# Attention passes of a two-layer decoder trunk: the second scores, the first maxima and the softmax scaling at other places in a hand-written order

## The chip, the cores and the metric

The kernel runs on one core of a Trainium2 chip. The metric is device time in microseconds (us) of one execution. The engines are named as in the profile: PE is the matrix engine and PEld its weight load, DVE the vector engine, ACT the scalar engine, POOL GpSimd, SP the engine that issues most loads.

## The reference

One sequence of 512 tokens, 1024 wide, goes through two layers. Layer 0 is a gated short convolution and a SwiGLU feed-forward part. Layer 1 is attention and the same kind of feed-forward part. The change touches the attention alone: 16 query heads of 64, four shared key/value heads, blocks of 128 queries that see their own block and the one before it, and a sink, one learned number a head that takes part in the softmax sum and not in the output.

```python
scores = einsum(q, k) / 8                      # per head: 4 blocks of 128 queries x 256 keys
scores = where(valid, scores, -1e30)           # sliding window of 128
probs = softmax(concat([scores, sink]))[..., :-1]
attn = einsum(probs, v) @ b_w_o
```

## The kernel before

All products are made in fp32 by splitting each operand into a high part (a rounded copy, made by ACT) and a low part (the difference, made by DVE), and adding three products: high times low, high times high, low times high. So each operand that PE multiplies costs one ACT and one DVE instruction, and each product three matmuls.

The attention works on head pairs: tile t of the queries holds heads 2t and 2t+1, and there are eight pairs. For one pair the steps are, with the letter that the order uses:

- **Q, R, H** project, rotate and split the queries (lines 1293 to 1305). The rotation reads PSUM on DVE (`sh`, `ra`, lines 1261 and 1263) and ends on POOL.
- **S0, S1** scores of the first and the second two query blocks (line 1319), twelve matmuls each, into two PSUM banks, one for each head of the pair.
- **M0, M1** maxima (line 1337): four DVE instructions each, that add the mask, write the scores `s` to SBUF and leave the negated row maximum in `nm`.
- **E00, E01, E10, E11** exponents (line 1353): four ACT instructions for each half, each with a read-out of its sum into `rs`, and two small ones with the sink's share `se`.
- **N0, N1** normalise (line 1371): DVE adds the sums, takes the reciprocal `rd` and multiplies the four pieces of `s` by it.
- **T0 to T3** turn (line 1384): PE transposes the probabilities into a PSUM bank `pt` of a pool of two. **P0 to P3** are the high copies `phi` or `lp` on ACT, **L0 to L3** the low parts `plo` or `lp` on DVE.
- **W0 to W3** weigh (line 1410): PE multiplies by the values into two banks `po`. **O** joins the two heads' results (line 1422: two ACT copies, then two DVE additions into `o`), and **o** splits the joined tile (line 1431: `ohl` or `ohi` and `olo`).
- **Z, z** work on the output projection of the first four pairs (line 1447: twelve matmuls into a bank `pe`, copied out by ACT). **G** and **g** split weights (`whi` on ACT, `wlo` on DVE).

The table ORDER (line 47) is walked once for each pass i of the loop at line 1539, i from 0 to 9. All instructions go to the engines' queues in the order in which the walk comes to them, each engine works off its queue in order, and an instruction at the head of a queue that waits holds up all behind it. In pass i, S, M, E and N work on pair i; T, P, L and W on pair i-1; a letter with a minus behind it (R-, O-, o-, H-) belongs to the pass before, so O- and o- work on pair i-2. Q works on pair i+2, R- and H- on pair i+1. Z starts in pass 5, when four pairs are joined, with two units in each of the passes 5 to 8, so that pass 5 has both the last Q and the first two Z. The passes 4 and 6 split more weights than the others.

NEXT (line 50) names the passes in which S1 is moved up to stand directly behind S0 (line 1548). There S1 takes its banks from the pool `ps_mm` of four, which also holds `pq`, `po` and `pe` (line 1322). In pass 5 and in pass 8 (which has no pair) it isn't moved; in pass 5, S1 stands behind P1 and reuses the two banks of `ps_sc` that M0 has read.

Of the kernel before, what the change touches and what calls it, by code (L numbers as in the profile page):

```python
# [10 lines left out]
F32 = mybir.dt.float32  # L11
F32R = mybir.dt.float32r
AF = mybir.ActivationFunctionType
ALU = mybir.AluOpType
PSUM = bass.MemoryType.PSUM

P = 128
# [27 lines left out]

EARLY_IN, REST_IN = 2, 0
ORDER = (
    "R- S0 T0 T1 O- Q0 M0 Q1 o- Z0 P0 P1 S1 T2 T3 L0 Q2 L1 G M1 E00 E01 k H- g0 Q3 P2 P3 E10 E11 Z1 z0 W0 L2 L3 A A A N0 W1 W2 N1 W3 g1 z1"
)
NEXT = (0, 1, 2, 3, 4, 6, 7)  # L50
STEP = {
    "S": "scores", "M": "maxima", "E": "exponents", "N": "normalise", "T": "turn", "P": "high",
    "L": "low", "W": "weigh", "O": "join", "o": "out", "Q": "project", "R": "rotate", "H": "split",
# [4 lines left out]
EARLY = 4  # L58
# [16 lines left out]
def yoco_kernel(  # L75
# [22 lines left out]
    nc = tc.nc  # L98
# [7 lines left out]
    small = ctx.enter_context(tc.tile_pool(name="small", bufs=3))  # L106
# [7 lines left out]
    def name(s):  # L114
        uid[0] += 1
        return f"{s}_{uid[0]}"
# [13 lines left out]
    def bank(s, pool=None):  # L130

        if pool is None:
            pool = (ps_mm, ps_sc, ps_mm, ps_pt)[turn[0] % 4]
            turn[0] += 1
        return pool.tile([P, S], F32, tag="bank", name=name(s))
# [421 lines left out]
    for l in range(2):  # L557
# [3 lines left out]
        for rd, (f0, f1) in enumerate(ROUNDS[:-1]):  # L561
            k = slice(f0 // 2, f1 // 2)
# [4 lines left out]
    def sum_on(at):  # L567

        issue(len(issues))
        if at in BEGIN:  # L570
            summing.append(sums_of[BEGIN[at]])
        for x in summing:
            x.step()
        summing[:] = [x for x in summing if x.steps]
# [390 lines left out]
    def first_weights(l):  # L965
        return ([w_gu[l, f, j] for f in range(2) for j in range(2)]
                + [w_gb[l, 0, b] for b in range(2)])
# [298 lines left out]
    def rope_turn(sh, eng):  # L1266
        eng.tensor_tensor(out=sh, in0=sh, in1=stab, op=ALU.mult)
# [10 lines left out]
    def rope_split(a, eng, large=False):  # L1278
        hi, lo = halves("rhl", F32R) if large else (slot("rhi", F32R), slot("rlo", F32R))
        nc.scalar.activation(hi, a, AF.Copy)  # L1280
        eng.tensor_tensor(out=lo, in0=a, in1=hi.bitcast(F32), op=ALU.subtract)
        return hi, lo
# [24 lines left out]
    class Heads:  # L1307
# [11 lines left out]
        def scores(self, half):  # L1319
            khi, klo = ks[self.t // 4]  # L1320
            qhi, qlo = qs[self.t].hi, qs[self.t].lo
            pool = ps_mm if half and self.t in NEXT else ps_sc
            self.pss[half] = pss = [bank("psc", pool) for _ in range(2)]
# [28 lines left out]

        def exponents(self, half, i):
            pe, nm = self.pe[half], self.nm[half]
            if i == 0:
                se = small.tile([P, 2, 2], F32, tag="se", name=name("se"))
                rs = small.tile([P, 2, 2], F32, tag="rs", name=name("rs"))
                self.sums[half] = se, rs
            se, rs = self.sums[half]
            cc = self.spans(half)[i][1]  # L1360
            for e in range(2):
                nc.scalar.activation(
                    pe[e][:, cc], pe[e][:, cc], AF.Exp, bias=nm[:, e, i : i + 1],
                    scale=-1.0, accum_out=rs[:, e, i : i + 1],
                )
            if i == 1:
                for e in range(2):
                    h = 2 * self.t + e
                    nc.scalar.activation(se[:, e], nm[:, e], AF.Exp, bias=snk[:, h : h + 1])

        def normalise(self, half):
            se, rs = self.sums[half]
            pe = self.pe[half]
            nc.vector.tensor_tensor(out=se, in0=se, in1=rs, op=ALU.add)
            rd = small.tile([P, 2, 2], F32, tag="rd", name=name("rd"))
            nc.vector.reciprocal(out=rd, in_=se)
            for i, cc in self.spans(half):
                for e in range(2):
                    nc.vector.tensor_scalar(
                        out=pe[e][:, cc], in0=pe[e][:, cc], scalar1=rd[:, e, i : i + 1],  # L1380
                        scalar2=None, op0=ALU.mult,
                    )
# [81 lines left out]
    with tc.manual_schedule(engines=ALL):  # L1464
# [20 lines left out]
        for hf in range(2):  # L1485
            c = slice(hf * 256, (hf + 1) * 256)
# [44 lines left out]
        for j in range(NB):  # L1531
            if j == 2:
                qs[0].split(nc.vector)
            nc.vector.tensor_tensor(out=dst[j][:, :, 1:3], in0=src[j],
                                    in1=dst[j][:, :, 0::3].bitcast(F32), op=ALU.subtract)

    with tc.manual_schedule(engines=ALL):
        sum_on("a0")
        for i in range(KT + 2):
            if i == KT:  # L1540
                res = Update(mix_o, B_ATT, [G_FPRE[1]])
                res.leaves = True
                ahead = Ahead(first_weights(1))
            if i == KT + 1:
                res.load()
            order = ORDER
            if i in NEXT:
                order = order.replace("S1 ", "").replace("S0 ", "S0 S1 ")
            for c in order.split():
                if c == "A":  # L1550
                    if i == KT:
                        ahead.one()
                    continue
                if c == "k":
                    if i == 3:
                        ks.append(rope_split(rot_k, nc.gpsimd))
                    continue
                late = c.endswith("-")
                op, n = c[0], [int(d) for d in c[1:].rstrip("-")]
                t = i - late  # L1560
                if op == "g":

                    u = 2 * (t - EARLY - 1) + n[0]
                    if u in (-2, -1, 2, 3):
                        j = u + 2 if u < 0 else u
                        early_w.append(split_weights(w_o[j // 2, j % 2], slots=j >= EARLY_IN))
                    continue
                if op in "SMENTPLWOo":
                    t -= op in "TPLWOo"
                    of = hp  # L1570
                elif op in "QRH":
                    t += LEAD
                    of = qs
                elif op == "G":
                    t += LEAD + 1
                    of = qs
                    if KT <= t < KT + 4:
                        j = t - KT
                        rest_w.append(split_weights(w_o[j // 2, 2 + j % 2], slots=j >= REST_IN))
                else:  # L1580
                    t = 2 * (t - EARLY - 1) + n.pop(0)
                    of = early
                if 0 <= t < len(of) and not (op in "RH" and t < LEAD - 1):
                    getattr(of[t], STEP[op])(*n)
                if op == "H" and i == 1:
                    rope_turn(begun_k[0], nc.gpsimd)
                if op == "H" and i == 2:
                    rot_k = rope_add(*begun_k, nc.gpsimd)
                if op in "RH" and i <= KT:
                    issue(len(issues) // 2 if op == "R" else len(issues))  # L1590
            if i <= KT:
                sum_on(f"a{i + 1}")
        close(rest_w, at, EARLY, res, ahead, lambda: sum_on(f"a{KT + 2}"), 1)
# [96 lines left out]
```

## Time and profile before

| what | value |
| --- | --- |
| median of 3 runs | 1024.36 us (1023.87 to 2562.63) |
| profiled execution, its time | 1024.8 us |
| its span | 1021.9 us (2.9 us lie around it) |
| PE busy | 1005.3 us, 98% of the span |
| DVE busy | 879.1 us, 86% |
| ACT busy | 589.6 us, 58% |
| POOL busy | 190.2 us, 19% |
| pass 0 begins (first `sh` of the walk) | 547.59 us |
| last W of the passes ends, first matmul of the part behind | 660.16 us |

The passes thus take 112.6 of the 1021.9 us. Ahead of them PE is busy without a gap, and behind them begins the rest of the output projection (`pmix`) and then the second feed-forward part. In the tables of the profile each row of a timeline has the start in us, the length in us, the engine, the line, the operation, the tile written and those read, the shape, and how many instructions were merged; a bracket behind a row is the time the engine stood idle before it and what ended that. A length includes the overlap with the next instruction, so what an instruction costs its queue is read from the start of one row to the start of the next.

### The profile page before, as it was taken

The numbers are of one execution on the slowest core, as the hardware profiler recorded it, in microseconds if no ns is written. First come the engines' busy times: TensorE is split into PE (matmuls) and PEld (weight loads), VectorE is DVE, ScalarE is ACT, GpSimd is POOL, SyncE is SP. The second block draws the span as 40 slices with busy tenths as digits, with TensorE's granted clock in tenths as the row PEclk, the third lists the DMA queues.
The fourth block names the chain that finished last, engine by engine and source line by source line (L and its number), as shares of the span: only waits on it lengthen the run. The fifth ranks groups of instructions, "written<-read, shape, count | busy, mean of one in ns | idle before, by whom it ended". The sixth has DMA issues, their size and how long they took to land.

```text
span 1021.9 us, 16136 instructions
## 1 busy us (share of the span) xinstructions
PE 1005.3 (98%) x5944; PEld 888.4 (87%) x5944; DVE 879.1 (86%) x1496; ACT 589.6 (58%) x1051; POOL 190.2 (19%) x251
## 2 busy tenths in 40 slices
PE   9999999999999999999999899999999999999997
PEld 8888888999889898998898777789998998989986
DVE  5766767899789989999879999888997899999896
ACT  6323445875655454656476678768566564645641
POOL 0443033112111111100114553221211010110001
PEclk9999999999999999999999999999999999999999
DMA  9897689559979699779405889976899676979742
GB/s 359 288 268 223 182 250 347 150 168 286 346 242 299 201 304 342 215 224 327 167 22 149 191 246 235 255 264 165 249 306 320 184 236 221 287 289 257 264 159 83
DMA packets 66575, 244.50 MB, mean 239 GB/s; under 512 B 7872, under 2 KB 8384, under 8 KB 54720
## 3 DMA queue, kind: packets, MB, share of 16 engines
q1 hardware_dynamic: 51328, 145.98, 38.4%
q0 software_dynamic: 14592, 96.48, 37.6%
q10 hardware_dynamic: 576, 1.02, 0.3%
q8 instruction: 46, 0.75, 0.3%
q14 instruction: 33, 0.27, 0.1%
HBM read 237.15 MB, written 102.76 MB: 333 GB/s over the span
## 4 chain that ended last, share of the span: by engine, by line
PE 91%; DVE 7%; ACT 2%; issue 0%; DVEq 0%; ACTq 0%
PE gx L1072 14%; PE gx L1075 7%; PE gz L195 4%; PE gz L193 4%; PE gz L194 4%; PE pcub L194 4%; PE pcub L193 4%; PE pcub L195 4%; PE px L194 4%; PE px L193 4%; PE px L195 4%; PE pmix L195 3%; PE pmix L193 3%; PE pmix L194 3%; PE gy L194 2%; PE gy L193 2%
## 5 line engine op out<-in xcount | busy, mean ns | idle before, releaser
L479 DVE TENSOR_TENSOR wlo<-raw,whi 128x1024 fp32r<-128x1024 f32 x225 | 274.7, 1225 | 53.0 <-ACT whi L478 52.8
L478 ACT ACTIVATE whi<-raw 128x1024 fp32r<-128x1024 f32 x225 | 233.7, 1051 | 100.4 <-DVE raw L466 28.8
L1072 PE MATMUL gx<-xt,whi 128*128 128x512 f32 x480 | 120.4, 393 | 0.0
L1072 PEld LDWEIGHTS gx<-xt,whi 128*128 128x128 f32 x480 | 86.2, 189 | 15.6
L547 POOL DMA_DIRECT2D hsum<-in_w_gb_dram x96 | 62.9, 734 | 152.9 <-ACT whi L478 90.0
L1034 DVE TENSOR_TENSOR st<-gx,st 128x256 f32<-128x256 f32 x200 | 78.0, 419 | 2.5 <-ACT st L1050 0.4
L1050 ACT ACTIVATE st<-gx 128x256 f32<-128x256 f32 x120 | 43.5, 380 | 62.3 <-PE gx L1075 58.6
L547 POOL DMA_DIRECT2D hsum<-hsum x32 | 25.4, 793 | 289.8 <-ACT whi L478 219.3
L1075 PEld LDWEIGHTS gx<-xt,wlo 128*128 128x128 f32 x480 | 65.5, 190 | 4.7
L1075 PE MATMUL gx<-xt,wlo 128*128 128x256 f32 x480 | 66.9, 282 | 0.0
L1086 ACT ACTIVATE gr<-gr 128x1024 f32<-128x1024 f32 x20 | 21.2, 1062 | 50.1 <-DVE gr L1034 50.1
L193 PE MATMUL px<-wlo,ahi 128*128 128x512 f32 x120 | 46.7, 389 | 0.0
L194 PE MATMUL px<-whi,ahi 128*128 128x512 f32 x120 | 46.7, 389 | 0.0
L195 PE MATMUL px<-whi,alo 128*128 128x512 f32 x120 | 46.7, 389 | 0.0
L195 PE MATMUL gz<-xhi,wlo 128*128 128x256 f32 x160 | 45.5, 284 | 0.0
L193 PE MATMUL gy<-xlo,whi 128*128 128x256 f32 x160 | 45.3, 283 | 0.0
L194 PE MATMUL gy<-xhi,whi 128*128 128x256 f32 x160 | 45.3, 283 | 0.0
L193 PE MATMUL gz<-xt,whi 128*128 128x256 f32 x160 | 45.3, 283 | 0.0
L194 PE MATMUL gz<-xt,whi 128*128 128x256 f32 x160 | 45.3, 283 | 0.0
L193 PE MATMUL gz<-xlo,whi 128*128 128x256 f32 x160 | 45.3, 283 | 0.0
L195 PE MATMUL gz<-xt,wlo 128*128 128x256 f32 x160 | 45.3, 283 | 0.0
L195 PE MATMUL gy<-xhi,wlo 128*128 128x256 f32 x160 | 45.3, 283 | 0.0
(293 smaller groups left out, 2969.5 us busy)
## 6 DMA issues: line engine op xcount, KB each, us to landing
hsum<-in_w_gb_dram POOLq DMA_DIRECT2D x96, 512.0 KB, 7.6
raw<-hsum SPq DMA_DIRECT2D x88, 512.0 KB, 8.0
raw<-in_w_gb_dram SPq DMA_DIRECT2D x60, 512.0 KB, 7.1
hsum<-in_w_dn_dram POOLq DMA_DIRECT2D x36, 512.0 KB, 8.1
raw<-in_w_dn_dram SPq DMA_DIRECT2D x32, 512.0 KB, 5.9
hsum<-hsum POOLq DMA_DIRECT2D x28, 512.0 KB, 5.7
raw<-in_w_in_dram SPq DMA_DIRECT2D x21, 512.0 KB, 7.4
hsum<-in_w_dn_dram POOLq DMA_DIRECT2D x12, 768.0 KB, 10.3
```

The costliest lines, as they stand in the source:

```text
L193: nc.tensor.matmul(out, whi, xlo, start=start, stop=False, **kw)
L194: nc.tensor.matmul(out, whi, xhi, start=False, stop=False, **kw)
L195: nc.tensor.matmul(out, wlo, xhi, start=False, stop=stop, **kw)
L478: self.begun = nc.scalar.activation(hi[:, :n], raw, AF.Copy)
L479: nc.vector.tensor_tensor(out=lo[:, :n], in0=raw, in1=hi[:, :n].bitcast(F32), op=ALU.subtract)
L547: nc.gpsimd.dma_start(dst, src, max_dma_last_dim=4 * 4 * S, **kw))
L1034: nc.vector.tensor_tensor(out=out, in0=a, in1=b, op=ALU.add)
L1050: nc.scalar.activation(ste, a, AF.Copy)
L1072: nc.tensor.matmul(banks[c][e], whi[:, kk], factors[p][k][2], start=opened and k == 0, stop=False, **kw)
L1075: nc.tensor.matmul(banks[c][e][:, :256], wlo[:, kk], factors[p][k][0], start=False, stop=k == 3 and p == 4, **kw)
L1086: nc.scalar.activation(kept[2], kept[2], AF.Silu)
```

## The change

Five edits, all in the attention passes:

1. NEXT is only pass 0. In the passes 1 to 4, 6 and 7, S1 now stands behind P1, with the banks of `ps_sc`.
2. O- (join) stands behind M0 instead of ahead of Q0 and M0, and o- (split of the joined tile) behind L0 instead of ahead of P0.
3. In the passes up to 5 the first output projection unit stands behind o- (as Y0) instead of ahead of P0. From pass 6 on it stays at Z0.
4. The sums `se`, `rs` and the reciprocal `rd` hold both halves of a pair in one tile of 128x8. N0 adds and inverts for both halves; N1 has no sum and no reciprocal of its own.
5. The four multiplications of the first half are ACT instructions with a scale operand; those of the second half stay on DVE.

```diff
--- before.py
+++ after.py
@@ -45,9 +45,9 @@
 
 EARLY_IN, REST_IN = 2, 0
 ORDER = (
-    "R- S0 T0 T1 O- Q0 M0 Q1 o- Z0 P0 P1 S1 T2 T3 L0 Q2 L1 G M1 E00 E01 k H- g0 Q3 P2 P3 E10 E11 Z1 z0 W0 L2 L3 A A A N0 W1 W2 N1 W3 g1 z1"
+    "R- S0 T0 T1 Q0 M0 O- Q1 Z0 P0 P1 S1 T2 T3 L0 o- Y0 Q2 L1 G M1 E00 E01 k H- g0 Q3 P2 P3 E10 E11 Z1 z0 W0 L2 L3 A A A N0 W1 W2 N1 W3 g1 z1"
 )
-NEXT = (0, 1, 2, 3, 4, 6, 7)
+NEXT = (0,)
 STEP = {
     "S": "scores", "M": "maxima", "E": "exponents", "N": "normalise", "T": "turn", "P": "high",
     "L": "low", "W": "weigh", "O": "join", "o": "out", "Q": "project", "R": "rotate", "H": "split",
@@ -1352,11 +1352,10 @@
 
         def exponents(self, half, i):
             pe, nm = self.pe[half], self.nm[half]
-            if i == 0:
-                se = small.tile([P, 2, 2], F32, tag="se", name=name("se"))
-                rs = small.tile([P, 2, 2], F32, tag="rs", name=name("rs"))
-                self.sums[half] = se, rs
-            se, rs = self.sums[half]
+            if half == i == 0:
+                self.sums = [small.tile([P, 2, 2, 2], F32, tag=s, name=name(s))
+                             for s in ("se", "rs")]
+            se, rs = (x[:, half] for x in self.sums)
             cc = self.spans(half)[i][1]
             for e in range(2):
                 nc.scalar.activation(
@@ -1369,13 +1368,19 @@
                     nc.scalar.activation(se[:, e], nm[:, e], AF.Exp, bias=snk[:, h : h + 1])
 
         def normalise(self, half):
-            se, rs = self.sums[half]
             pe = self.pe[half]
-            nc.vector.tensor_tensor(out=se, in0=se, in1=rs, op=ALU.add)
-            rd = small.tile([P, 2, 2], F32, tag="rd", name=name("rd"))
-            nc.vector.reciprocal(out=rd, in_=se)
+            if half == 0:
+                se, rs = self.sums
+                nc.vector.tensor_tensor(out=se, in0=se, in1=rs, op=ALU.add)
+                self.rd = small.tile([P, 2, 2, 2], F32, tag="rd", name=name("rd"))
+                nc.vector.reciprocal(out=self.rd, in_=se)
+            rd = self.rd[:, half]
             for i, cc in self.spans(half):
                 for e in range(2):
+                    if half == 0:
+                        nc.scalar.activation(pe[e][:, cc], pe[e][:, cc], AF.Copy,
+                                             scale=rd[:, e, i : i + 1])
+                        continue
                     nc.vector.tensor_scalar(
                         out=pe[e][:, cc], in0=pe[e][:, cc], scalar1=rd[:, e, i : i + 1],
                         scalar2=None, op0=ALU.mult,
@@ -1555,6 +1560,9 @@
                     if i == 3:
                         ks.append(rope_split(rot_k, nc.gpsimd))
                     continue
+                if c == ("Z0" if i <= EARLY + 1 else "Y0"):
+                    continue
+                c = c.replace("Y", "Z")
                 late = c.endswith("-")
                 op, n = c[0], [int(d) for d in c[1:].rstrip("-")]
                 t = i - late
```

The end of pass 3 (pair 3), DVE before: `se`, `rs` and `rd` are the sums and reciprocals, `s` the probabilities.

```order
L1374 TENSOR_TENSOR se_6199<-se_6199,rs_6200 128x4
L1376 RECIPROCAL rd_6241<-se_6199 128x4
L1379 TENSOR_SCALAR s_6151<-s_6151,rd_6241 128x128
L1379 TENSOR_SCALAR s_6152<-s_6152,rd_6241 128x128
L1379 TENSOR_SCALAR s_6151<-s_6151,rd_6241 128x256
L1379 TENSOR_SCALAR s_6152<-s_6152,rd_6241 128x256
L1374 TENSOR_TENSOR se_6224<-se_6224,rs_6225 128x4
L1376 RECIPROCAL rd_6256<-se_6224 128x4
L1379 TENSOR_SCALAR s_6193<-s_6193,rd_6256 128x256
L1379 TENSOR_SCALAR s_6194<-s_6194,rd_6256 128x256
L1379 TENSOR_SCALAR s_6193<-s_6193,rd_6256 128x256
L1379 TENSOR_SCALAR s_6194<-s_6194,rd_6256 128x256
```

DVE of the change at the same place:

```order
L1374 TENSOR_TENSOR se_6184<-se_6184,rs_6185 128x8
L1376 RECIPROCAL rd_6224<-se_6184 128x8
L1384 TENSOR_SCALAR s_6178<-s_6178,rd_6224 128x256
L1384 TENSOR_SCALAR s_6179<-s_6179,rd_6224 128x256
L1384 TENSOR_SCALAR s_6178<-s_6178,rd_6224 128x256
L1384 TENSOR_SCALAR s_6179<-s_6179,rd_6224 128x256
```

and ACT of the change, from the sink's exponents on:

```order
L1368 ACTIVATE se_6184<-nm_6177,snk 128x2 x2
L1381 ACTIVATE s_6117<-s_6117,rd_6224 128x128
L1381 ACTIVATE s_6118<-s_6118,rd_6224 128x128
L1381 ACTIVATE s_6117<-s_6117,rd_6224 128x256
L1381 ACTIVATE s_6118<-s_6118,rd_6224 128x256
L1431 ACTIVATE o_6297<-po_6215 64x512
L1431 ACTIVATE o_6297<-po_6216 64x512
L1409 ACTIVATE phi_6274<-pt_6269 128x512
L1409 ACTIVATE phi_6281<-pt_6276 128x512
L1441 ACTIVATE ohl_6335<-o_6297 128x512
```

Six DVE rows are gone, the one sum stands behind the exponents of both halves, and the first half's multiplications stand on ACT ahead of the two copies of the join; the split of the joined tile follows the two `phi` copies.

The start of pass 4 on DVE, before (the rotation, the join, and the first of the four maxima):

```order
L1261 STREAM_SHUFFLE sh_6266<-pq_6143 128x512
L1263 TENSOR_TENSOR ra_6268<-pq_6143,ctab_5215 128x512
L1428 TENSOR_TENSOR o_6317<-po_6232,o_6317 64x512
L1428 TENSOR_TENSOR o_6317<-po_6233,o_6317 64x512
L1346 ISA s_6330,nm_6329<-psc_6275,mask,nsnk 128x128
```

and of the change, from the third of the four maxima on (the rotation and the first two stand ahead of it):

```order
L1346 ISA s_6291,nm_6290<-psc_6255,mask,nsnk 128x256
L1346 ISA nm_6290 128x1
L1346 ISA s_6292,nm_6290<-psc_6256,mask,nsnk 128x256
L1346 ISA nm_6290 128x1
L1433 TENSOR_TENSOR o_6297<-po_6215,o_6297 64x512
L1433 TENSOR_TENSOR o_6297<-po_6216,o_6297 64x512
L1413 TENSOR_TENSOR plo_6275<-pt_6269,phi_6274 128x512
L1442 TENSOR_TENSOR ohl_6335<-o_6297,ohl_6335 128x512
L1413 TENSOR_TENSOR plo_6282<-pt_6276,phi_6281 128x512
```

The join `o` has moved from ahead of the four maxima to behind them, and the first low part `plo` from behind the split `ohl` to ahead of it.

PE in pass 5, before: the end of the first output projection unit (`pe`), and the start of S1.

```order
L193 MATMUL pe_6517<-wlo_6451,ohl_6514 128x512
L194 MATMUL pe_6517<-whi_6450,ohl_6514 128x512
L195 MATMUL pe_6517<-whi_6450,ohl_6514 128x512
L1334 MATMUL psc_6532<-rlo_6208,rhl_6386 128x256
L1334 MATMUL psc_6533<-rlo_6208,rhl_6386 128x256
```

The change has there S1's last matmuls, the transposes of T2 and T3 (`pt`), and behind them the start of the unit:

```order
L1334 MATMUL psc_6491<-rhi_6192,rhl_6366 128x256
L1334 MATMUL psc_6492<-rhi_6192,rhl_6366 128x256
L1396 MATMUL pt_6505<-ident,s_6352 128x128 x2
L1396 MATMUL pt_6505<-ident,s_6353 128x128 x2
L1396 MATMUL pt_6512<-ident,s_6352 128x128
L1396 MATMUL pt_6512<-ident,s_6353 128x128
L193 MATMUL pe_6519<-wlo_6375,ohl_5992 128x512
L194 MATMUL pe_6519<-whi_6374,ohl_5992 128x512
L195 MATMUL pe_6519<-whi_6374,ohl_5992 128x512
```

The unit stood ahead of S1, T2 and T3, and now stands behind them.

## The prediction

> **What bounds the kernel now.** I read the page first: the busy shares, then the chain that ended last.
>
> ```profile
> PE 1005.3 (98%) x5944; PEld 888.4 (87%) x5944; DVE 879.1 (86%) x1496; ACT 589.6 (58%) x1051; POOL 190.2 (19%) x251
> PE 91%; DVE 7%; ACT 2%; issue 0%; DVEq 0%; ACTq 0%
> ```
>
> PE bounds the program, and DVE holds 7% of the chain. The change touches only the attention passes, so next I cut the trace into passes, from one `sh` (or join) to the next. These are the passes 1 to 6; the columns are length, then busy time of PE, PEld, DVE, ACT and POOL with counts, then PE's granted clock.
>
> ```profile
> 556.55:567.08 10.53, 10.03 (x67) 8.61 (x66) 10.39 (x37) 8.95 (x28) 7.86 (x8) 1.00 0.83 206
> 567.08:581.08 14.00, 12.65 (x78) 10.94 (x78) 13.06 (x40) 9.58 (x29) 7.49 (x7) 0.88 0.84 207
> 581.08:594.21 13.13, 11.12 (x79) 9.56 (x78) 12.69 (x40) 10.11 (x31) 6.95 (x7) 1.00 0.83 169
> 594.21:610.06 15.85, 14.51 (x90) 12.62 (x91) 14.77 (x42) 11.59 (x31) 7.47 (x9) 0.89 0.80 250
> 610.06:622.59 12.53, 12.10 (x66) 9.67 (x65) 12.25 (x41) 8.91 (x30) 5.41 (x5) 1.00 1.02 312
> 622.59:639.05 16.46, 15.02 (x121) 13.00 (x119) 15.21 (x46) 14.33 (x39) 6.50 (x7) 1.00 0.91 209
> ```
>
> Here DVE is the fullest engine (12.69 of 13.13 us in pass 3), so its queue comes close to setting the pass. The waits of the same stretch (us in total, times, longest) tell what PE and ACT stand for:
>
> ```profile
> ACT ohl L1436 <- DVE o L1428: 12.3, 4, 3.7
> PE psc L1334 <- DVE ra L1263: 5.2, 3, 2.0
> ```
>
> S1 waits 5.2 us for the rotation (its second bank was `pq`'s). PE has other slack in these passes, so what counts is when DVE and ACT finish. Pass 3 on DVE, and then on ACT:
>
> ```profile
> 581.08 0.72 DVE L1261 STREAM_SHUFFLE sh<-pq 128x512 f32<-128x512 f32 x1
> 582.29 1.40 DVE L1428 TENSOR_TENSOR o<-po,o 64x512 f32<-64x512 f32 x2
> 583.72 0.35 DVE L1346 CUSTOM_DVE_ANT_0 s<-psc,mask,nsnk 128x128 f32<-128x128 f32 x1
> 585.08 0.69 DVE L1437 TENSOR_TENSOR ohl<-o,ohl 128x512 fp32r<-128x512 f32 x1
> ...
> 591.82 1.01 DVE L1379 TENSOR_SCALAR s<-s,rd 128x128 f32<-128x128 f32 x4
> 592.74 0.15 DVE L1374 TENSOR_TENSOR se<-se,rs 128x4 f32<-128x4 f32 x1
> 593.14 1.14 DVE L1379 TENSOR_SCALAR s<-s,rd 128x256 f32<-128x256 f32 x4
> 594.21 0.01 DVE L1261 LOAD_MASK_SELECT sh<-pq  x1
> ```
>
> ```profile
> 583.72 0.63 ACT L1436 ACTIVATE ohl<-o 128x512 fp32r<-128x512 f32 x1 [2.52 <-DVE o L1428]
> 584.26 1.07 ACT L1404 ACTIVATE phi<-pt 128x512 fp32r<-128x512 f32 x2
> 585.22 1.06 ACT L188 ACTIVATE whi<-raw 128x1024 fp32r<-128x1024 f32 x1
> 586.16 0.40 ACT L1362 ACTIVATE s<-s,nm 128x128 f32<-128x128 f32 x1
> ...
> 588.29 0.63 ACT L1280 ACTIVATE rhi<-ra 128x512 fp32r<-128x512 f32 x1
> 588.81 0.63 ACT L1280 ACTIVATE rhl<-ra 128x512 fp32r<-128x512 f32 x1
> 589.33 0.59 ACT L1404 ACTIVATE phi<-pt 128x512 fp32r<-128x512 f32 x1
> 590.07 0.51 ACT L1362 ACTIVATE s<-s,nm 128x256 f32<-128x256 f32 x1
> ...
> 592.55 1.21 ACT L1426 ACTIVATE o<-po 64x512 f32<-64x512 f32 x2
> ```
>
> ACT has no gap from the split of the joined tile (583.72) to the end of the second exponents (592.55), 8.83 us, and the second half's sum (592.74) follows at once. Two limits stand side by side: DVE's queue, and a ring through ACT. Until the second exponents are done, DVE fills its time with the first half's normalising (591.82 to 592.74 and its sum before).
>
> **The change part by part.** Edits 4 and 5 take six instructions a pair off DVE. In pass 3 the multiplications are 592.74 - 591.82 = 0.92 us, the sum and reciprocal 593.14 - 592.74 = 0.40: 1.32 us a pair, 10.6 us over eight. But the one sum now waits for the exponents of both halves, so DVE has nothing to fill that wait with: behind it in DVE's queue stand the second half's multiplications (T1 waits for them), the next rotation (POOL waits) and M0, and ACT's scaling and so T0 wait for its reciprocal. That is the wait the change adds. ACT gets four instructions with a scale operand. The nearest rows are one such instruction on 128x256 and an exponent on 128x128:
>
> ```profile
> 695.53 1.57 ACT L351 ACTIVATE xhl<-xt,gt 128x256 fp32r<-128x256 f32 x4 [0.67 <-PE xt L338]
> 586.46 0.20 ACT L1362 ACTIVATION_READ_ACCUMULATOR s<-s,nm 128x1 f32 x1
> ```
>
> Four of the first take 1.57, so about 0.37 each from start to start and a little over at the end; the second kind starts its read-out 0.30 after its own start at 586.16. Two of 0.37 and two of 0.29 make 1.32 us. From below, half a 128x512 copy (two `phi` in 584.26 to 585.22, so 0.24 for a half) gives 0.96 for four; from above, the whole first exponents with their read-outs and the sink's share, 586.16 to 588.29, give 2.13. I take 1.32, since the 128x256 row is the same kind of instruction.
>
> Now the ring of a pass in the change, from reciprocal to reciprocal, each link from the rows above: second half's multiplications 1.07 (593.14 to 594.21), rotation 1.21, maxima 1.36, join 1.43 (edit 2 puts the maxima into the ring), then on ACT split 0.54, `whi` 0.94, first exponents 2.13, `rhl` 0.52, `phi` and `lp` 0.74 (589.33 to 590.07), second exponents 2.48, and the sum and reciprocal 0.40. That is 12.82 us. The two `phi` copies (0.96) have left the ring, ahead of the split; the scaling (1.32) lies in the time in which ACT waits for the join, 2.52 us in the row at 583.72, and costs nothing there. If that cover were gone it would add its 1.32.
>
> - Pass 2: 14.00 becomes 12.82, -1.18.
> - Pass 3 has `rhi` as well (0.52): 13.34 for 13.13, +0.21.
> - Pass 1 has no join; its ring is scaling 1.32, T0 0.55 (half of eight transposes, 1.09 in a row below), `phi` 0.96, then 0.94 + 2.13 + 0.52 + 0.74 + 2.48 + 0.40, together 10.04 for 10.53: -0.49.
> - Pass 4 splits two more weights.
>
> ```profile
> 602.73 1.05 ACT L188 ACTIVATE whi<-raw 128x1024 fp32r<-128x1024 f32 x1
> 608.92 1.22 DVE L189 TENSOR_TENSOR wlo<-raw,whi 128x1024 fp32r<-128x1024 f32 x1
> ```
>
> The first adds 0.95 to the ring. The last `whi` now stands behind the scaling, and DVE's last `wlo` (1.14 to the next `sh`) waits for it: from the reciprocal 1.32 + 1.05 + 1.14 = 3.51 instead of 1.07, +2.44. Pass 4: 12.82 + 0.95 + 2.44 = 16.21 for 15.85, +0.36.
>
> So pass 5 starts 1.1 us earlier, at 608.95. Pass 5 is PE's:
>
> ```profile
> 616.15 0.87 PE L1391 MATMUL pt<-ident,s 128*128 128x128 f32 x6
> 616.78 0.47 PE L193 MATMUL pq<-xlo,whi 128*128 128x512 f32 x1
> 619.61 0.39 PE L193 MATMUL pe<-wlo,ohl 128*128 128x512 f32 x1
> 622.33 0.40 PE L1417 MATMUL po<-phi,vt 128*128 128x256 f32 x2
> 624.34 0.39 PE L1334 MATMUL psc<-rlo,rhl 64*128 64x256 f32 x2
> ```
>
> Before, the first unit filled PE while T2 and T3 waited for their `pt` banks. With edit 3 it stands behind T3, and T3's bank is free when L1 is done: rotation 1.21, maxima 1.36, join 1.43, then three DVE instructions of 0.6 (585.08 is the first of their kind), 5.8 us into the pass, 614.76. A third of the transposes 0.2, the unit 2.72, Q2 and Q3 2.83, the second unit 2.72 and W 2.01 end at 625.24, where before they ended at 624.34: +0.9. The lead of 1.1 is gone into PE's wait for L0 and L1, which is what comes late next. S1, which no longer stands behind S0, is made up later in the same pass. M0 waits for S0 and the join now stands behind M0. Pass 6 has the tail of pass 4 again (the last `whi` behind the scaling), +0.36; the passes 7 and 8 I take as even. Sum: +0.9 + 0.36 = +1.3 us.
>
> The profiled execution took 1024.8 us (span 1021.9 and 2.9 around it), the median shown is 1024.36; on it the forecast is 1025.7 us. With scaling at 0.96 or 2.13 the two tails move it by -0.7 or +1.6. The 5.2 us of S1's wait I count as no gain: PE then waits for the scaling instead, in the same slack. No moved step issues a DMA; the loads of weights, which SP issues when a `wlo` has freed a buffer, move with their pass by tenths of a us, and none is in the rows of waits that carry this sum.
>
> One edit is checked against a rule. These rows follow S1's waits of 1.84 and 1.34 us:
>
> ```profile
> 568.43 0.38 PE L1334 MATMUL psc<-rlo,rhl 64*128 64x256 f32 x1 [1.84 <-DVE ra L1263]
> 569.59 1.97 PE L1391 MATMUL pt<-ident,s 128*128 128x128 f32 x8
> ...
> 582.43 0.38 PE L1334 MATMUL psc<-rlo,rhl 64*128 64x256 f32 x1 [1.34 <-DVE ra L1263]
> 583.32 1.09 PE L1391 MATMUL pt<-ident,s 128*128 128x128 f32 x8
> ```
>
> After 1.84 us eight transposes took 1.97 us, after 1.34 us 1.09, and the granted clock of that pass is 0.88. The Trainium skill (TensorE: Matmul & The Clock Gate, section on the HAM clock gate) gives half rate only after an idle window of about 3.4 us. By that rule no wait here would slow PE and the slower rival below would have no price; the trace does not agree, and the sum goes by the rows.
>
> **The rivals.**
>
> *PE's new wait makes it slow (slower).* Behind the P3 copy S0 still needs two low parts (0.6 and half of that), a quarter of W (0.5) and its own matmuls (0.9, from 582.43 to 583.32), an estimate of 2.3 us; the scaling ends 2.48 + 0.40 + 1.32 = 4.2 us behind that copy. So T0 waits some 1.9 us, above the 1.84 that was followed by slow transposes. Each time costs 1.97 - 1.09 = 0.9 us. It decides only where PE is last, from pass 5 on; in four passes 3.5 us on top of the forecast: 1029.2. Against it: in pass 5 and 6 PE arrives late itself.
>
> *The lead of pass 5 is kept.* If the unit's delay is taken up because PE has slack behind it (12.10 of 12.53 busy in pass 5 speaks against that, 15.02 of 16.46 in pass 6 for it), the 1.1 us arrive: 1023.3.
>
> *DVE's queue alone was the bound.* Then its 10.6 us come in full: 1013.8. For it: DVE at 97% of pass 3. Against it: ACT's 8.83 us without a gap, into which the new sum runs.
>
> *The change does not do what it says*, in that S1 still waits: its banks are free after M0, 2.6 us into the pass, and PE comes to it after T0, T1, Q0 and Q1, later than that, so it hardly can be; and if S1 did wait as before, the time would be the ring's all the same, 1025.7, since S1's wait is counted at nothing. It has no chance of its own.
>
> **How the numbers follow.** Forecast 1025.7: 0.58. Slower 1029.2: 0.17. Lead kept 1023.3: 0.17. DVE alone 1013.8: 0.08. The range reaches from 1020.5 (short of the last) to 1029.5, which leaves out that case and about half of the slow one's upper side, under 2 in 10. The forecast's own range is 1024.5 to 1027. About 2%, 20 us, is what a measurement of this kernel can tell from no change; no case reaches it. Faster 0.01, within 0.98, slower 0.01.
>
> **What would show it.** Right: DVE busy about 868 us and ACT about 600; the wait of `psc` for `ra` gone; the sum (L1374) idle for ACT by about 2 us a pair; T0 waiting for ACT's scaling; passes 2 and 3 near 12.8 and 13.3 us; in pass 5 the transposes waiting for `plo`; the passes ending near 661.4. Wrong: passes of 11 us (the ring isn't closed by the sum), or transposes of 1.97 us in the passes 5 to 8.

## The result, and the profile after

The change took 1028.83 us, the median of five executions (1027.65 to 1030.66); the kernel before, run beside it, 1023.87. The ratio is 1.0052, with a 95% interval from 1.0035 to 1.0068: slower by 5.0 us. The forecast was 1025.7, 3.1 us less, and its range ended at 1029.5. That the kernel would be a little slower was right; the size, +1.3 us, was not.

The page's busy line of the kernel after:

```profile
PE 1007.9 (98%) x5944; PEld 886.4 (86%) x5944; DVE 868.9 (84%) x1448; ACT 601.9 (58%) x1083; POOL 189.6 (18%) x251
```

DVE lost 10.2 us of work and ACT gained 12.3, as the edits say. Next the passes 1 to 5, from `sh` to `sh`, and the sixth from its `sh` to the join of the seventh (length, then busy time of PE, PEld, DVE, ACT and POOL, then PE's clock):

```profile
558.75:569.31 10.56, 10.42 (x67) 8.68 (x69) 9.15 (x31) 9.36 (x32) 7.74 (x8) 1.00 0.86 216
569.31:582.17 12.86, 12.36 (x91) 10.07 (x89) 11.11 (x36) 11.08 (x35) 7.51 (x7) 1.00 0.83 214
582.17:595.55 13.38, 11.77 (x78) 9.37 (x78) 11.11 (x34) 11.60 (x36) 6.83 (x7) 1.00 0.79 176
595.55:611.97 16.42, 14.49 (x92) 11.44 (x93) 13.72 (x36) 14.60 (x39) 7.50 (x9) 1.00 0.82 252
611.97:625.31 13.34, 10.72 (x50) 8.27 (x49) 11.26 (x35) 10.42 (x34) 5.36 (x5) 0.87 1.03 290
625.31:647.23 21.92, 20.58 (x137) 17.14 (x136) 15.75 (x47) 16.45 (x45) 8.88 (x11) 1.00 0.73 177
```

Passes 2 and 3 are what the forecast said (12.82 and 13.34; in pass 3 no engine is busy for more than 11.8 of the 13.4 us), and pass 5 starts only 0.26 us earlier against pass 0 than before (62.21 us behind it, where it was 62.47). From there the time is lost. The first scores of pass 6 (S0, at 629.82) start 80.06 us behind pass 0, before 76.75, so 3.31 us; from S0 to the end of the span it is 399.08 us where it was 397.56, another 1.52. Together 4.83 us. All of it lies in the passes, which end 117.5 us behind pass 0 (at 667.24) where it was 112.6.

The span grew by 7.0 us, not 4.8, since pass 0 starts 2.2 us later (549.76 for 547.59). For the greater part that was lost near 285 us, in code that the change doesn't touch, where ACT waited for a load: this row stands among its waits, 5.3 us in two waits, the longer of 4.0 (a second execution of the same kernel, below, shows 3.1 and 2.6).

```profile
ACT whi L478 <- DMA raw<-hsum: 5.3, 2, 4.0
```

So the passes are measured from pass 0 on below. The waits in them (us in total, times, longest):

```profile
DVE se L1374 <- ACT se L1368: 8.7, 8, 1.6
ACT ohl L1441 <- DVE o L1433: 6.4, 4, 2.8
PE pt L1396 <- DVE plo L1413: 4.7, 7, 1.0
DVE s L1346 <- PE psc L1334: 4.2, 1, 4.2
PE pt L1396 <- ACT s L1381: 4.1, 10, 0.8
```

The wait of `psc` for `ra` is gone. The sum waits for ACT in each of eight pairs, about 1.1 us a pair. The fourth row is new: in pass 6 DVE stands 4.22 us at M0 until S0 has run, and the join stands behind it. DVE there:

```profile
630.84 0.35 DVE L1346 CUSTOM_DVE_ANT_0 s<-psc,mask,nsnk 128x128 f32<-128x128 f32 x1 [4.22 <-PE psc L1334]
...
632.19 1.41 DVE L1433 TENSOR_TENSOR o<-po,o 64x512 f32<-64x512 f32 x2
```

and ACT's half of that join:

```profile
629.82 1.21 ACT L1431 ACTIVATE o<-po 64x512 f32<-64x512 f32 x2 [1.20 <-PE po L1422]
```

It ended at 631.03, so the join could have begun there and began 1.16 us later. Pass 5 on PE, the second place where time goes:

```profile
614.37 0.76 PE L1334 MATMUL psc<-rlo,rhl 64*128 64x256 f32 x2 [0.94 <-DVE nm L1346]
...
616.73 0.66 PE L1396 MATMUL pt<-ident,s 128*128 128x128 f32 x4 [1.01 <-DVE plo L1413]
618.00 0.69 PE L1396 MATMUL pt<-ident,s 128*128 128x128 f32 x2 [0.61 <-DVE plo L1413]
618.34 0.78 PE L193 MATMUL pe<-wlo,ohl 128*128 128x512 f32 x1
...
622.38 0.39 PE L193 MATMUL pq<-xlo,whi 128*128 128x512 f32 x1
...
629.82 0.39 PE L1334 MATMUL psc<-rlo,rhl 64*128 64x256 f32 x2
```

PE stands idle three times within 4.6 us (613.43 to 618.00), then the unit's first matmuls take 0.78 and 0.63 us instead of 0.39, and the unit takes 4.04 us (618.34 to 622.38) where 2.72 was counted.

### The profile page after: what moved, and what is told of

Its sections match the earlier page's. It is cut to its first block, busy times and chain, and to the rows that moved or that the text cites. A ratio compares the mean times of both kernels' runs of the same rounds, so it can differ in the third digit from the quotient of the medians.

```text
span 1028.9 us, 16145 instructions
## 1 busy us (share of the span) xinstructions
PE 1007.9 (98%) x5944; PEld 886.4 (86%) x5944; DVE 868.9 (84%) x1448; ACT 601.9 (58%) x1083; POOL 189.6 (18%) x251
## 5 line engine op out<-in xcount | busy, mean ns | idle before, releaser
L194 PE MATMUL gz<-xhi,whi 128*128 128x256 f32 x160 | 45.3, 283 | 0.0
```

Source lines behind the costliest of these rows:

```text
L194: nc.tensor.matmul(out, whi, xhi, start=False, stop=False, **kw)
```

## The experiments

Three causes could account for the loss. Theory 1: the unit that was moved in pass 5 leaves PE idle there. Theory 2: the scaling on ACT with its one sum. Theory 3: the maxima ahead of the join. In this part edit 2 means the join behind the maxima alone, and the later place of the joined tile's split is counted with edit 3, since the unit needs the split. First, three kernels that undo one edit and one that makes one edit alone. For each kernel the table at the end gives the medians and three lengths from its trace.

### The unit and the split back at their places (edit 3 undone)

```diff
-Q0 M0 O- Q1 Z0 P0 P1 S1 T2 T3 L0 o- Y0 Q2
+Q0 M0 O- Q1 o- Z0 P0 P1 S1 T2 T3 L0 Q2
```

> The change, but with the split of the joined tile and the first output unit of pass 5 back at their old places, ahead of the first copies. Theory 1 (the loss is made in pass 5, where PE stands in front of the waiting transposes with nothing to do and its clock drops): the unit fills PE again, the transposes of pass 6 start 2.6 us earlier against the start of pass 0, so about 1026.2 us, and no matmul of the unit takes over 0.45 us. Theory 2 (the loss is made by the scaling on ACT with its one sum): no gain, 1028 to 1029. Theory 3 (maxima ahead of the join delays the join in the passes 6 to 8): no gain either, 1028 to 1029.

It took 1032.22 us (ratio to before 1.0092, 1.0077 to 1.0107): 9.0 us over the kernel before, where the change is 5.0 over it. All three expectations miss, theory 1's by its sign. It is half right all the same: pass 5, from `sh` to the S0 of the next pass, is 14.91 us instead of 17.85. But edit 3 also moves the split of the joined tile in every pass, and with the split early the passes 2 to 4 are 0.96 to 0.98 us longer each (13.84, 14.34 and 17.40), and the time from S0 of pass 6 to the end is 401.67 instead of 399.08. From pass 0 to the end this trace is 7.4 us over the kernel before; its pass 0 also starts 2.4 us later, behind code that no edit touches. The split ahead of the low parts holds up DVE and ACT until the join is done; with the join first it costs nearly as much (edits 2 and 3 undone together, below).

### The join ahead of the maxima (edit 2 undone for the join)

```diff
-T1 Q0 M0 O- Q1
+T1 O- Q0 M0 Q1
```

> The change, but with the join ahead of the maxima on DVE, as before. Theory 3 (in the passes 6 to 8 the maxima wait for scores that PE makes last, and the join, which is ready, stands behind them): the 1.2 to 1.4 us per pass come back in part, about 1027 us; the passes 2 to 4 get up to 1.36 us shorter each if ACT's ring holds them, and that lead is lost again at pass 5. Theory 1 (all in pass 5's unit): 1028 to 1029. Theory 2 (scaling on ACT with its one sum): 1028 to 1029.

It took 1023.69 us (ratio 1.0001, 0.9993 to 1.0010), no longer measurably slower than the kernel before. The loss is gone: theory 3, and more of it than theory 3 had expected. The passes 2 to 5 of this kernel:

```profile
567.75:579.32 11.57, 11.57 (x88) 9.74 (x88) 10.95 (x36) 10.97 (x35) 7.51 (x7) 1.00 0.92 241
579.32:591.41 12.09, 11.91 (x87) 9.80 (x83) 10.96 (x36) 11.49 (x36) 6.88 (x7) 1.00 0.88 176
591.41:606.54 15.13, 14.75 (x93) 11.62 (x93) 13.31 (x38) 14.48 (x39) 7.47 (x9) 1.00 0.84 249
606.54:619.62 13.08, 10.65 (x50) 8.57 (x49) 11.10 (x37) 10.53 (x34) 5.33 (x5) 0.87 1.02 325
```

Each of the first three is 1.29 us shorter than in the change, the four maxima's 1.34 us within 0.05 (570.54 to 571.88 in the change's pass 2). ACT's timeline in pass 2 says why. In the change:

```profile
573.32 0.63 ACT L1441 ACTIVATE ohl<-o 128x512 fp32r<-128x512 f32 x1 [1.17 <-DVE o L1433]
```

With the join first:

```profile
570.46 0.63 ACT L1441 ACTIVATE ohl<-o 128x512 fp32r<-128x512 f32 x1
570.99 1.06 ACT L188 ACTIVATE whi<-raw 128x1024 fp32r<-128x1024 f32 x1
571.93 0.40 ACT L1361 ACTIVATE s<-s,nm 128x128 f32<-128x128 f32 x1
```

ACT needs the join first (for the split) and the maxima two instructions later (for the first exponents). With the join first, DVE makes the maxima while ACT splits, and the exponents start without a wait. With the maxima first, ACT stands still for the join (1.17 us), and then the maxima have long been done. With the join first PE is busy in all of pass 2's 11.57 us, so that the ring alone sets this pass is not shown.

### Each half's sum and scaling back on DVE (edits 4 and 5 undone)

```diff
-            if half == 0:
-                se, rs = self.sums
...
+            se, rs = self.sums[half]
...
+            rd = small.tile([P, 2, 2], F32, tag="rd", name=name("rd"))
...
-                    if half == 0:
-                        nc.scalar.activation(pe[e][:, cc], pe[e][:, cc], AF.Copy,
-                                             scale=rd[:, e, i : i + 1])
-                        continue
```

> The moves of the change alone: each half has its own sum and reciprocal again and the first half is scaled on DVE. Theory 2 (one sum and scaling on ACT cost the time, by DVE's idle wait for the second exponents and by the late last weight split of the passes 4 and 6): 1024 to 1026 us. Theory 1 (pass 5's unit behind the transposes): 1028 or more, since DVE then carries 1.3 us more a pass while the transposes still wait for it.

It took 1027.18 us (1.0036, 1.0024 to 1.0048), between the two expectations: a loss of 4.0 us instead of 5.0, and 1.5 us less than the change from pass 0 to the end: theory 2 holds a fifth to a third of the loss, not all of it. Up to S0 of pass 6 this kernel is as slow as the change (79.90 us behind pass 0, the change 80.06); the gain lies behind that, 397.77 us to the end instead of 399.08.

### One sum and scaling on ACT alone (edits 4 and 5 on the kernel before)

```diff
+            if half == 0:
+                se, rs = self.sums
...
-            se, rs = self.sums[half]
...
-            rd = small.tile([P, 2, 2], F32, tag="rd", name=name("rd"))
...
+                    if half == 0:
+                        nc.scalar.activation(pe[e][:, cc], pe[e][:, cc], AF.Copy,
+                                             scale=rd[:, e, i : i + 1])
+                        continue
```

> The kernel before with one sum per pair and the first half's scaling on ACT, and none of the moves. Theory 1 (pass 5's unit): 1022.5 to 1024.5 us, no loss, since the unit stands where it stood. Theory 2 (one sum and scaling on ACT): 1027 to 1029, most of the loss.

It took 1025.55 us (1.0021, 1.0013 to 1.0030), between the two expectations. The passes 1 to 5 gain 1.8 us (S0 of pass 6 at 74.95 us instead of 76.75) and all behind loses 3.7 (401.26 instead of 397.56). So the two edits save time in the passes that DVE and ACT set, and cost more than that behind them, all of it in pass 7. There S1 waits for a bank until ACT has copied out the second unit of pass 6 (`mixo`), and this copy now stands behind the scaling. PE stands idle for 2.54 us. The kernel before has this wait, too, but of 1.01 us:

```profile
637.61 0.58 PE L1334 MATMUL psc<-rlo,rhl 64*128 64x256 f32 x1 [2.54 <-ACT mixo L1459]
```

```profile
634.54 1.49 ACT L1381 ACTIVATE s<-s,rd 128x128 f32<-128x128 f32 x4
635.95 1.13 ACT L182 ACTIVATE whi<-raw 128x512 fp32r<-128x512 f32 x2
636.98 0.57 ACT L1459 ACTIVATE mixo<-pe 128x512 f32<-128x512 f32 x1
```

From S0 of pass 6 to this S1 it is 15.07 us where it was 13.53. Behind the wait PE is slow (last section), and up to T2 of pass 7 it is 7.50 us where it was 5.31. Together these are the 3.7 us; from T2 on both kernels take the same 378.7. T0's waits for the scaling (0.52 us in all behind S0 of pass 6) are not the cost here. In the change S1 takes other banks and this wait does not come up, so the price of the edits there is another one.

### Edits 2 and 3 undone together

```diff
-T1 Q0 M0 O- Q1 Z0 P0 P1 S1 T2 T3 L0 o- Y0 Q2
+T1 O- Q0 M0 Q1 o- Z0 P0 P1 S1 T2 T3 L0 Q2
```

> Edits 2 and 3 undone together: join ahead of the maxima, and the joined tile's split and the first output unit at their old places; S1 late, one sum and scaling on ACT stay. Theory 3 as it now stands (the maxima ahead of the join sit in front of everything that hangs on the join, 1.36 us a pass): pass 5 then starts some 4 us earlier against pass 0 than before (ring 11.5, 12.0 and 14.9 to 15.1 us in the passes 2 to 4) and the unit fills PE there, 1019.5 to 1022 us. Rival (PE is full from pass 5 on, so that a lead at pass 5 is worth nothing): 1023 to 1024.

It took 1024.51 us (1.0007, 0.9998 to 1.0016), above both expectations. The lead of 4 us at pass 5 didn't come, only 1.4 (61.03 us for 62.47): the passes 2 to 4 were 12.48, 12.99 and 16.04 us, 0.90 to 0.91 longer each than with the split late. The ring worked out for the expectation had left out that the early split costs these passes, too. Pass 5 took 14.25 us to the next S0, as before. In pass 7 of this trace PE was slow behind a wait of 1.24 us (six transposes in 1.49 us, and a granted clock of 0.88 from 638.68 to 652.45).

### The maxima ahead of the join alone (edit 2 on the kernel before)

```diff
-T1 O- Q0 M0 Q1 o- Z0
+T1 Q0 M0 O- Q1 o- Z0
```

> The kernel before with edit 2 alone: the maxima ahead of the join, all else as before. Theory 3: most of the loss, 1027 to 1030 us, with the passes 2 to 4 up to 1.36 us longer each and the join of the passes 6 to 8 waiting behind maxima that wait for PE. Rival (the order of join and maxima costs only together with the late unit): 1023 to 1024.5.

It took 1029.64 us (1.0059, 1.0046 to 1.0072): the one edit alone loses 5.75 us, no less than all five. Its passes 2 to 5, and its row of ACT's wait for the join, 12.3 us in the kernel before:

```profile
566.84:581.30 14.46, 11.51 (x78) 9.50 (x78) 13.22 (x40) 9.46 (x29) 7.48 (x7) 1.00 0.75 191
581.30:595.78 14.48, 13.13 (x71) 11.40 (x73) 12.79 (x40) 9.24 (x29) 6.94 (x7) 0.76 0.72 153
595.78:612.22 16.44, 14.59 (x102) 12.01 (x99) 14.79 (x42) 12.10 (x33) 7.48 (x9) 1.00 0.81 247
612.22:626.11 13.89, 12.90 (x70) 10.00 (x69) 12.44 (x43) 9.45 (x30) 5.47 (x5) 1.00 1.00 293
```

```profile
ACT ohl L1436 <- DVE o L1428: 17.6, 4, 5.0
```

The four passes are 0.46, 1.35, 0.59 and 1.36 us longer. With the join first nothing of this is left, so edit 2's part for the join is shown as the cause from both sides: put in alone it costs 5.75 us, and taken out alone it lowers the loss from 5.0 or 4.7 to 0.5 us (by 5.3 us in the traces from pass 0 on). Two more pairs in the table at the end differ by it alone: the kernel with edits 1, 2 and 3 and that with 1 and 3 (5.3 us from pass 0 on), and the kernel without edit 3 and that with 1, 4 and 5 (6.2 us).

### The scaling behind the last weight split

The kernel is the one with edits 2 and 3 undone, with the scaling in a step X0 of its own.

```diff
-N0 W1 W2 N1 W3 g1 z1
+N0 W1 W2 N1 W3 g1 X0 z1
...
+        def scale(self, half):
+            pe, rd = self.pe[half], self.rd[:, half]
+            for i, cc in self.spans(half):
+                for e in range(2):
+                    nc.scalar.activation(pe[e][:, cc], pe[e][:, cc], AF.Copy,
+                                         scale=rd[:, e, i : i + 1])
```

> As the kernel with edits 2 and 3 undone, and the first half's scaling on ACT put behind the copy for the last weight split (whi) instead of ahead of it; it differs in the passes 4 and 6 alone. Theory (the late split is what the scaling costs in these two passes, 1.4 us each): DVE's wait of wlo for whi at their ends falls from 1.39 and 0.96 us to under 0.3, and the time by 0.5 to 2 us against that kernel. Rival (T0 waits for the scaling instead, and PE is what counts): no gain, or up to 1 us slower.

It took 1022.93 us (0.9992, 0.9983 to 1.0001), 1.6 us less than the same kernel without the step, within the expectation. Pass 4 fell from 16.04 to 14.56 us, the 1.4 us expected, and `wlo` no longer waits at the ends of the passes 4 and 6. Part of the gain goes into T0, which now waits up to 0.93 us for the scaling. The two traces differ by 2.23 us from pass 0 to the end: 0.78 up to S0 of pass 6 and 1.45 behind it. Behind it this kernel has no slow stretch in pass 7 (clock 1.00 from 637.66 to 650.17), so how much of the gain is the copy's place and how much PE's clock isn't separated.

### The change once more

> The change unaltered. If the 2.2 us by which pass 0 started later (549.76 for 547.59) belong to that one execution, pass 0 starts at 547.5 to 548.5 here and the median is 1027.5 to 1028.5 us; if they belong to the change, it starts at 549.8 again and the median is 1029 to 1030.5. In both cases pass 0's start to the end of the span takes 479 us, where it was 474.3 before.

The median was 1028.58 us (1.0042, 1.0028 to 1.0056). Pass 0 started at 548.46, between the two, and from there to the end took 479.44 us (before 474.31), so the passes' loss of 5 us repeats to 0.3, and the 2.2 us ahead of them belong to that one execution for the greater part.

### The join first from pass 5 on only

```diff
             order = ORDER
+            if i > EARLY:
+                order = order.replace("Q0 M0 O-", "O- Q0 M0")
```

> The change, with the join ahead of the maxima from pass 5 on and the maxima ahead of the join in the passes 1 to 4 as the change has it. Theory A (from pass 5 on PE is full, so what the passes 2 to 4 save or lose is worth nothing, and the loss of 5 us is made in the passes 5 to 8): pass 5 starts 62.2 us behind pass 0 as in the change, and the time is 1023.5 to 1025 us, as with the join first everywhere. Theory B (the 3.9 us that the passes 2 to 4 lose to the maxima come through): 1026 to 1027.5.

It took 1027.58 us (1.0039, 1.0027 to 1.0052): theory B, and 0.1 us over its bounds. Pass 5 starts 62.20 us behind pass 0, with the join first everywhere 58.34; of these 3.86 us 3.63 are still there at S0 of pass 6 (79.56 and 75.93) and 3.56 at the end. A lead at pass 5 does come through; PE has waits there to give up. So of the 5.34 us that the join behind the maxima costs, 3.56 are made in the passes 1 to 4 and 1.78 from pass 5 on.

### Edits 1 and 3 alone

Against the change, beside the sums and the scaling as shown for the third kernel:

```diff
-T1 Q0 M0 O- Q1
+T1 O- Q0 M0 Q1
```

> The kernel before with edit 1 (second scores late) and edit 3 (the joined tile's split and the first output unit late) alone: join ahead of the maxima, each half with its own sum, first half scaled on DVE. Theory (edits 4 and 5 cost 1.2 to 1.9 us by the late weight splits and the idle wait of the one sum): 1021.5 to 1023 us, under the 1023.7 of the kernel with the join first. Rival (the one sum and the scaling on ACT are what pays for the late unit, since DVE is then 1.3 us a pass fuller): 1024 to 1026.

It took 1022.22 us (0.9986, 0.9977 to 0.9995), as the theory said. Beside the kernel with the join first it shows edits 4 and 5 once more: up to S0 of pass 6 they save 0.18 us, behind it they cost 1.57 (397.87 for 396.30).

### The join first, and the scaling behind the split

```diff
-T1 Q0 M0 O- Q1 Z0 ... W3 g1 z1
+T1 O- Q0 M0 Q1 Z0 ... W3 g1 X0 z1
```

> Edits 1, 3, 4 and 5 with the join ahead of the maxima, and the first half's scaling behind the copy for the last weight split. Theory (the two parts add up): 1.5 us under the 1023.7 of the kernel with the join first, so 1021.5 to 1022.5 us. Rival (PE has no room from pass 5 on and S1's wait for the first maxima, 2.38 us in pass 5, holds the time): 1023 to 1024.

It took 1020.59 us (0.9973, 0.9964 to 0.9982), 2.9 us faster than the kernel before and the best of all: the parts add up, and to more than expected: some 3 us under the kernel with the join first (2.80 in the traces) rather than 1.5. Pass 4 gives 1.48 of them, and pass 5 to the next S0 another 1.16 (S1 waits 0.62 us for the maxima there, in the other kernel 2.38, and PE's granted clock is 1.00 there, in the other kernel 0.87). The end of pass 4 in it, on DVE and on ACT:

```profile
602.28 0.20 DVE L1376 RECIPROCAL rd<-se 128x8 f32<-128x8 f32 x1
602.52 1.14 DVE L1382 TENSOR_SCALAR s<-s,rd 128x256 f32<-128x256 f32 x4
603.58 1.22 DVE L189 TENSOR_TENSOR wlo<-raw,whi 128x1024 fp32r<-128x1024 f32 x1
604.73 0.01 DVE L1261 LOAD_MASK_SELECT sh<-pq  x1
```

```profile
601.95 1.05 ACT L188 ACTIVATE whi<-raw 128x1024 fp32r<-128x1024 f32 x1
602.90 1.48 ACT L1391 ACTIVATE s<-s,rd 128x128 f32<-128x128 f32 x4
```

The copy runs while DVE makes the sum, and the low part follows the multiplications at once. In the change the same place reads:

```profile
608.29 1.14 DVE L1384 TENSOR_SCALAR s<-s,rd 128x256 f32<-128x256 f32 x4
610.82 1.23 DVE L189 TENSOR_TENSOR wlo<-raw,whi 128x1024 fp32r<-128x1024 f32 x1 [1.39 <-ACT whi L188]
```

### A quarter of the projection ahead of the second scores

```diff
-O- Q0 M0 Q1 Z0 ... Y0 Q2 L1
+O- Q0 M0 Q1 Q2 Z0 ... Y0 L1
```

> As that kernel, with the third quarter of the next query projection (Q2, 1.36 us on PE) ahead of the second scores, where PE waits 2.38 us for the first maxima in pass 5. If that wait is on the path that sets the end, the time falls by about 1.4 us more, to 1020 to 1021; if not, it stays within 0.5 us of that kernel. In the passes 1 to 4, where the second scores wait little, Q2 ahead of them can delay the transposes by up to 1.36 us; if those counted, it would be slower by 1 to 3 us.

It took 1020.76 us (0.9977, 0.9968 to 0.9986), the same time, which both first readings of the expectation allow. That decides little: pass 1 grew by 1.3 us (11.81 for 10.52) and pass 5 to the next S0 shrank by as much (15.07 for 16.43), so a gain and a loss cancelled. The expectation had named each of them, and not both together. The move in pass 5 alone was not run, nor was the version that these lengths point to, split late in all passes but early with its unit in pass 5.

### All kernels

"Loss" is the median less that of the kernel before on the same chip. The other columns are us from the traces: start of pass 5 behind pass 0, start of S0 of pass 6 behind pass 0, and from there to the end of the span.

| kernel | median | loss | pass 5 | S0 of pass 6 | from there |
| --- | --- | --- | --- | --- | --- |
| before | 1023.87 | | 62.47 | 76.75 | 397.56 |
| all five edits | 1028.83 | 5.0 | 62.21 | 80.06 | 399.08 |
| all five, again | 1028.58 | 4.7 | 62.22 | 80.31 | 399.13 |
| without 3 | 1032.22 | 9.0 | 65.13 | 80.04 | 401.67 |
| join first (1, 3, 4, 5) | 1023.69 | 0.5 | 58.34 | 75.93 | 397.87 |
| join first from pass 5 | 1027.58 | 4.1 | 62.20 | 79.56 | 397.80 |
| 1, 2, 3 | 1027.18 | 4.0 | 61.82 | 79.90 | 397.77 |
| 4, 5 | 1025.55 | 2.3 | 60.67 | 74.95 | 401.26 |
| 1, 4, 5 | 1024.51 | 0.6 | 61.03 | 75.28 | 400.20 |
| 1, 4, 5, scaling late | 1022.93 | -1.0 | 59.57 | 74.50 | 398.75 |
| 2 | 1029.64 | 5.8 | 64.87 | 79.80 | 400.05 |
| 1, 3 | 1022.22 | -1.2 | 58.42 | 76.11 | 396.30 |
| 1, 3, 4, 5, scaling late | 1020.59 | -2.9 | 56.83 | 73.26 | 397.74 |
| the same with Q2 early | 1020.76 | -2.7 | 58.30 | 73.37 | 397.64 |

Read along one path, the 4.83 us come apart: edits 1 and 3 give 1.90 (0.64 up to S0, 1.26 behind), edits 4 and 5 on top cost 1.39 (-0.18 and +1.57), and the join behind the maxima on top of these costs 5.34 (4.13 and 1.21). The shares hold for this path: put on the kernel before alone, edits 4 and 5 cost 1.90 in the traces (-1.80 and +3.70) and edit 2 costs 5.54. Edits 1 and 3 were not run apart.

## Why the prediction was right or wrong

**The bound, ACT's ring: right.** Passes of 12.82 and 13.34 us were forecast for the passes 2 and 3, 12.86 and 13.38 came, and without the maxima in the ring (11.46 and 11.98 by the same rows) 11.57 and 12.09. The four scalings take 1.40 us on ACT where 1.32 was taken (608.35 to 609.75), and in the passes 2 and 3 they lie in ACT's idle time, as said. The sum's wait for ACT came as 1.1 us a pair and not 2.

**Pass 1: wrong by 0.5 us.** The step gave 10.04 by the ring; PE is busy 10.42 of the 10.56 us that came. PE's share of that pass had stood in the rows shown (10.03 of 10.53). With 0.2 us more at the end of pass 4 (16.42 for 16.21), the lead at pass 5 was 0.26 us and not 1.1.

**Pass 5: right in the order of events, too small in its size.** The step gave +0.9 us at S0 of pass 6; +3.31 came. Of the 2.4 us between, 0.84 are the lead that wasn't there, 0.36 T2's and T3's later start and length, and 1.32 the unit at a slow clock; Q2 and Q3 gave back 0.1. The slower rival had that price of a wait, but put it at T0, which waited 0.4 us on average, 0.8 at most (4.1 us in ten waits), and was not slow. Nor does a wait above 1.84 us always make PE slow (last section). Its 1029.2 is near the result by chance: it counted four passes, and one was hit.

**S1's bank: wrong in the word "hardly".** In pass 5 S1 did wait for the maxima, 0.94 us. T2 and T3 waited for `plo` in any case, so this wait can have cost time only as a part of PE's idle time ahead of the slow unit; no run shows that by itself.

**Passes 6 to 8: the step that failed outright.** The +0.36 for pass 6 and "the passes 7 and 8 I take as even" stand against +1.52. The join behind the maxima is 1.21 of what is lost there, as the kernel with the join first shows, and edits 4 and 5 are 1.57; edits 1 and 3 give 1.26 back. PE's waits show where: from S0 of pass 6 to the end of the passes they add up to 4.27 us (3.06 for `plo`, 1.21 for the scaling) where they were 2.95. The prediction saw that M0 waits for S0 with the join behind it, and named no price. The rows at 630.84 and 632.19 have it, a join 1.16 us late in pass 6.

**What it saw without drawing the conclusion.** That "edit 2 puts the maxima into the ring" was in the sum, and the ring against before came out at -1.1 us over the passes 1 to 4, so the edit was never priced by itself. It costs 1.29 us in each of the passes 2 to 4 and 5.3 us in all. The other four edits without it are worth nothing measurable (+0.5 us), and with the scaling moved behind the split they are worth 2.9.

**The rivals.** DVE's queue alone is refuted: its work fell by 10.2 us and the time rose. "The lead of pass 5 is kept" had no lead to keep; but the last experiments show that it would have been kept (3.6 of 3.9 us).

## What to carry to other kernels

Of two instructions in one queue, put that one first whose reader comes first in its own queue: ACT asked for the join two instructions before it asked for the maxima, and the other way round cost 5.3 us. Price each edit by itself against the ring, not only the sum, since a small sum here held gains and losses several times its size; and carry each moved step through every pass it runs in, also those that another engine seems to bound.

## What the runs showed of the hardware

PE slowed after some short waits, and not after others as long. After the three idle times of 0.94, 1.01 and 0.61 us in pass 5 (within 4.6 us) its 128x512 matmuls took 0.63 to 0.78 us instead of 0.39, and the stage's granted clock is 0.87. The second execution had the same waits to 0.03 us, and there the slow matmuls began only with the unit's fourth (617.66). After a single wait of 2.38 us (join first, pass 5) and of 2.54 us (edits 4 and 5 alone, pass 7, the row at 637.61 above):

```profile
610.37 0.81 PE L1334 MATMUL psc<-rlo,rhl 64*128 64x256 f32 x2 [2.38 <-DVE nm L1346]
...
612.19 1.54 PE L1396 MATMUL pt<-ident,s 128*128 128x128 f32 x6
613.38 0.78 PE L193 MATMUL pe<-wlo,ohl 128*128 128x512 f32 x1
```

```profile
639.18 1.97 PE L1396 MATMUL pt<-ident,s 128*128 128x128 f32 x8
```

Six transposes in 1.54 us and eight in 1.97 are near half rate (0.87 and 1.09 in rows of the kernel before); the waits of 0.3 to 0.8 us ahead of T0 in the change were followed by no such row. Neither were waits of 1.82 us (edit 2 alone, pass 2), 1.87 (edits 4 and 5 alone, pass 4) and 2.25 (edit 3 undone, pass 7), though the kernel before was slow after 1.84:

```profile
652.02 1.04 PE L1396 MATMUL pt<-ident,s 128*128 128x128 f32 x6 [2.25 <-DVE plo L1413]
652.81 0.48 PE L193 MATMUL pe<-wlo,ohl 128*128 128x512 f32 x1
```

So the length of a single wait doesn't decide it alone. The Trainium skill (TensorE: Matmul & The Clock Gate, section on the HAM clock gate) has half rate after an idle window of about 3.4 us. No wait in the passes of these kernels was so long; the longest was 2.96 us (edit 2 alone, pass 3), and slow rows followed it. What does decide, no run here separates.
